# Sums of up-projection weights in five small steps and over more stages, and the next chunk's blocks among the last products

## The chip, the cores and the metric

One program on one core of a Trainium2 chip. The core has a matrix engine (TensorE, in the profile PE for its products and PEld for loading its weights), a vector engine (VectorE, DVE), a scalar engine (ScalarE, ACT), a third elementwise engine that also issues DMAs (GpSimd, POOL) and a sync engine (SyncE, SP) that here issues all loads of weights. The metric is the device time of one execution in microseconds (us); lower is better.

## The reference

One layer of a decoder for a prompt of 2048 rows and eight single sample rows, all in float32, width 1024. What matters, cut:

```python
def trunk_layer(x, ...):
    z = rmsnorm(x, g_mix) @ w_in            # pool 512 | q 512 | k 512 | v 512
    # group A: trailing means over 2, 4, 8, 16 rows; group B: differential attention, 4 heads, ALiBi
    o = attend(q, k, v, lam)                # softmax(q1 k1) - lam * softmax(q2 k2), times v
    x = x + concat([pool_out, rmsnorm(o)]) @ w_out
    x = x + cross_attn(rmsnorm(x, g_cross), mem_k, mem_v, wq_c, wo_c)     # 256 memory tokens
    f = conv_ffn(rmsnorm(x, g_ffn), conv_prefix, w_up, conv_w, conv_b, w_down)
    return x + f
def conv_ffn(h, prefix, w_up, conv_w, conv_b, w_down):
    up = h @ w_up                           # 1024 -> 2 * 2816, halves a | g
    c = causal_conv3(concat([prefix, up])) + conv_b
    return (silu(c_g) * c_a) @ w_down
```

The kernel also returns keys, values, memory keys and values, and the new pooling and convolution states.

## The kernel before, in words

**Numbers.** A float32 value is kept as two parts for the matrix engine, hi (a cast on ACT, `xhi`, `shi`, `whi`, L95 and L308) and lo (value minus hi, on DVE, `xlo`, `slo`, `wlo`, L96 and L311); a product is three matrix products, hi·hi, hi·lo and lo·hi.

**Stages.** The prompt is cut into four chunks of 512 rows and a few. In the profiled execution the stages follow each other so: memory keys and values and the first norm (0 to 90 us), input projection of chunks 0 and 1 (90 to 300), input projection of chunks 2 and 3 woven with the attention of chunks 0 and 1 (300 to 655), attention of chunks 2 and 3 woven with the output projection and first cross-attention work (655 to 1150), the rest of cross-attention together with the sample rows (1150 to 1640), and the feed-forward part, chunk by chunk (1640 to 3164, some 380 us a chunk).

**Feed-forward.** The 22 up-projections of a chunk go in groups of 4, 4, 4, 4, 4 and 2 (`GROUPS`). One up-projection (`ffn_up`, L1612 and L1614) yields an activation block and a gate block for two halves of the rows; instead of eight block products it makes seven, of sums and differences of blocks, in the manner of Strassen's algorithm. For this it needs (1) sums and differences of weight blocks, the same for all four chunks, and (2) seven blocks made from the chunk's normalized rows. The down-projections of a group (`down`, L1728, eight items of 12 products each) are spread among the products of the group behind it; those of a chunk's last group go among the first products of the next chunk.

**Weight sums** (`sums_items`). For each of the 22 up-projections a pair of tiles `wa`, `wg` (512 KB each) is loaded by SP (L1520), added and subtracted in four instructions on DVE (`add`, L1528 to L1531), split into hi and lo (`part`: per tile an ACT cast `shi`, L95, and a DVE subtraction `slo`, L96), and the four results are stored to DRAM tiles `s_d` by POOL's queue (L1540). The feed-forward part loads these back (`shl<-s_d`). A pair's load is recorded one pair ahead of its `add`. Eight pairs are woven into the input projection of chunks 0 and 1, fourteen into that of chunks 2 and 3 with the attention.

**Blocks of the next chunk** (`xop_items`). Seven items make the blocks: 14 tiles `xhi`/`xlo` of 128x512 and eight subtractions (L1572) on DVE. They stand behind the last up-projection of a chunk, in one run.

**What sets the order.** The order list at the end of the program is a list of items. `weave(main, extra, lo, hi)` spreads the items of `extra` over `main` by the cost of `main`'s items and the last number of each item of `extra`, from share `lo` to share `hi` of `main`. `drive` then records item by item, staging weights ahead (`look` says how many; load, then cast, then subtraction, L305, L308, L311). Each engine runs its instructions in the recorded order. All large tiles come from one pool of 41 buffers (`H`), so that a load on SP waits until the buffer that it takes is free, and every load behind it on SP waits with it. The loads of the attention's keys, values and queries (`K`, `V`, `Q`, L1073 to L1084) stand in the same queue.

## Time and profile before

| | us |
|---|---|
| median of three runs | 3166.14 |
| lowest and highest run | 3156.91, 3173.37 |
| the profiled execution | 3165.44 |
| its span, first to last instruction | 3163.7 |

The span lies 1.7 us below the time of the profiled execution. A row of the profile that names a group reads: line, engine, operation, tile written, tiles read and shape, then count, busy time, mean of one, and the idle time of the engine just ahead of these instructions with what ended it. A timeline row reads: start, duration, engine, line, operation, tiles, and in brackets the idle time before it with the instruction that ended it. The granted clock of TensorE (`PEclk`) is given as a share of full speed.

### The profile page before, as it was taken

The numbers are of one execution on the slowest core, as the hardware profiler recorded it, in microseconds if no ns is written. First come the engines' busy times: TensorE is split into PE (matmuls) and PEld (weight loads), VectorE is DVE, ScalarE is ACT, GpSimd is POOL, SyncE is SP. The second block draws the span as 40 slices with busy tenths as digits, with TensorE's granted clock in tenths as the row PEclk, the third lists the DMA queues.
The fourth block names the chain that finished last, engine by engine and source line by source line (L and its number), as shares of the span: only waits on it lengthen the run. The fifth ranks groups of instructions, "written<-read, shape, count | busy, mean of one in ns | idle before, by whom it ended". The sixth has DMA issues, their size and how long they took to land.

```text
span 3163.7 us, 52554 instructions
## 1 busy us (share of the span) xinstructions
PE 2958.2 (94%) x19806; PEld 2662.8 (84%) x19806; DVE 2244.5 (71%) x4032; ACT 1350.8 (43%) x2271; POOL 506.9 (16%) x961
## 2 busy tenths in 40 slices
PE   7999898879899998999989999999999999999998
PEld 6778787868889787679978989888898989899997
DVE  5744766556767668654568977887878777777777
ACT  5534444345665542333334343444434433443333
POOL 0244334321111115330000000000000010000100
PEclk9999999989999999999999999999999999999999
DMA  8797778843353356655449877677776786666762
GB/s 287 264 330 235 241 239 275 286 156 130 111 163 101 107 175 236 204 174 182 167 150 338 291 245 231 198 258 257 236 236 213 224 288 213 210 212 220 238 223 95
DMA packets 520513, 683.16 MB, mean 216 GB/s; under 512 B 27472, under 2 KB 342359, under 8 KB 520243
## 3 DMA queue, kind: packets, MB, share of 16 engines
q1 hardware_dynamic: 466525, 533.87, 52.2%
q0 software_dynamic: 39936, 135.17, 11.9%
q10 hardware_dynamic: 13798, 10.76, 1.0%
q8 instruction: 156, 2.56, 0.3%
q14 instruction: 98, 0.80, 0.1%
HBM read 549.12 MB, written 130.98 MB: 215 GB/s over the span
## 4 chain that ended last, share of the span: by engine, by line
PE 69%; DVE 9%; DMA 7%; issue 6%; ACT 2%; POOL 1%; SPq 0%; DVEq 0%; ACTq 0%; POOLq 0%
PE up L1612 14%; PE down L1728 14%; PE up L1614 7%; PE wo L484 4%; PE O L1164 3%; PE z L484 3%; PE sc L1112 3%; DMA wg<-in_w_up_dram 3%; PE upB L1612 2%; PE S L100 2%; PE S L102 2%; PE S L101 2%; PE vo L100 2%; PE vo L101 2%; PE vo L102 2%
## 5 line engine op out<-in xcount | busy, mean ns | idle before, releaser
L1728 PE MATMUL down<-act,whi 128*128 128x512 f32 (+1 forms) x1760 | 456.0, 353 | 11.8 <-ACT whi L308 8.4
L1612 PE MATMUL up<-xhi,shl 128*128 128x256 f32 (+1 forms) x2816 | 406.7, 286 | 5.1 <-ACT s L1627 1.8
L1612 PEld LDWEIGHTS up<-xhi,shl 128*128 128x128 f32 x2816 | 369.5, 189 | 37.1 <-ACT s L1627 11.2
L1666 ACT ACTIVATE cc<-Uf,vec 128x512 f32<-128x512 f32 (+1 forms) x176 | 144.0, 818 | 528.4 <-DVE Uf L1617 520.8
L311 DVE TENSOR_TENSOR wlo<-wraw,whi 128x1024 fp32r<-128x1024 f32 x256 | 308.6, 1218 | 38.8 <-ACT whi L308 26.4
L1728 PEld LDWEIGHTS down<-act,whi 128*128 128x128 f32 x1760 | 285.1, 189 | 43.3 <-ACT whi L308 9.3
L308 ACT CAST whi<-wraw 128x1024 fp32r<-128x1024 f32 x256 | 265.0, 1047 | 131.8 <-DMA wraw<-in_w_down_dram 30.0
L1728 PE MATMUL down<-act,wlo 128*128 128x512 f32 (+1 forms) x880 | 283.2, 353 | 7.5 <-DVE wlo L311 7.5
L1671 POOL COPY halo<-Uf 128x2 f32<-128x2 f32 x176 | 59.2, 336 | 1312.9 <-DVE Uf L1617 1273.1
L1130 ACT ACTIVATE T<-T,mn 128x1024 f32<-128x1024 f32 (+4 forms) x192 | 172.0, 897 | 143.0 <-DVE mn L1123 134.0
L1614 PE MATMUL up<-xlo,shl 128*128 128x256 f32 (+1 forms) x1408 | 225.1, 282 | 0.0
L1112 PE MATMUL sc<-K,Q 128*128 128x512 f32 (+5 forms) x640 | 178.0, 397 | 50.4 <-DVE mn L1123 44.8
L1612 PE MATMUL up<-xhi,whl 128*128 128x256 f32 (+1 forms) x1408 | 200.1, 285 | 5.1 <-DVE whl L330 3.0
L1612 PEld LDWEIGHTS up<-xhi,whl 128*128 128x128 f32 x1408 | 184.3, 190 | 13.9 <-DVE whl L330 5.2
L1614 PEld LDWEIGHTS up<-xlo,shl 128*128 128x128 f32 x1408 | 192.2, 189 | 0.2
L1674 DVE SCALAR_TENSOR_TENSOR cc<-Uf,vec,cc 128x512 f32<-128x512 f32 x176 | 131.5, 747 | 75.9 <-ACT cc L1666 75.8
L1617 DVE TENSOR_TENSOR Uf<-up,s 128x256 f32<-128x256 f32 (+1 forms) x264 | 111.6, 423 | 102.7 <-PE up L1614 100.7
L1728 PEld LDWEIGHTS down<-act,wlo 128*128 128x128 f32 x880 | 155.1, 189 | 31.7 <-DVE wlo L311 10.7
L330 DVE TENSOR_TENSOR whl<-wraw,whl 128x512 fp32r<-128x512 f32 x264 | 178.9, 684 | 0.2
L1112 PEld LDWEIGHTS sc<-K,Q 128*128 128x128 f32 x640 | 114.8, 201 | 73.1 <-DVE mn L1123 54.6
L484 PE MATMUL z<-h1hi,wlo 128*128 128x512 f32 (+1 forms) x480 | 163.7, 374 | 9.9 <-DVE mn L1123 5.4
L1732 DVE TENSOR_TENSOR xf<-xf,down 128x512 f32<-128x512 f32 (+1 forms) x240 | 135.0, 579 | 48.5 <-PE down L1728 46.7
(437 smaller groups left out, 7136.4 us busy)
## 6 DMA issues: line engine op xcount, KB each, us to landing
shl<-s_d SPq DMA_DIRECT2D x352, 512.0 KB
wraw<-in_w_up_dram SPq DMA_DIRECT2D x264, 256.0 KB
wraw<-in_w_down_dram SPq DMA_DIRECT2D x88, 512.0 KB
s_d<-shi POOLq DMA_DIRECT2D x44, 512.0 KB, 6.0
s_d<-slo POOLq DMA_DIRECT2D x44, 512.0 KB, 6.6
wraw<-in_w_in_dram SPq DMA_DIRECT2D x32, 512.0 KB
Q<-q_d SPq DMA_DIRECT2D x64, 256.0 KB
wraw<-in_w_out_dram SPq DMA_DIRECT2D x32, 512.0 KB
```

The costliest lines, as they stand in the source:

```text
L308: S.copy(self.hi[:, :1024], self.raw[:, :1024])
L311: V.tensor_tensor(self.lo[:, :1024], self.raw[:, :1024], f(self.hi[:, :1024]), ALU.subtract)
L330: V.tensor_tensor(self.hl[:, 512:1024], self.raw, f(self.hl[:, :512]), ALU.subtract)
L484: PE.matmul(out, w[wi][:, kt, :], kslice(z, kt, c0, n), start=i == 0, stop=i == 3 * KT - 1)
L1112: PE.matmul(ps[:, j * 512:j * 512 + w], v3(Q[c], 2)[:, z, self.t * P:(self.t + 1) * P], K[c][hf][:, c0:c0 + w], start=z == 0, stop=z == 1)
L1130: S.activation(tg[:, :mg], tg[:, :mg], AF.Exp, bias=mn[:, last:last + 1], scale=-1.0, accum_out=self.l[:, 2 * g + c:2 * g + c + 1])
L1612: PE.matmul(out, wi[:, k, :], xh[:, k], start=k == 0 and wi is wl, stop=False)
L1614: PE.matmul(out, wh[:, k, :], xl[:, k], start=False, stop=k == 3)
L1666: S.activation(cc[:, :w], U[:, 2:2 + w], AF.Identity, bias=vc(CB + nt), scale=vc(CWT + 2 * FT + nt))
L1674: V.scalar_tensor_tensor(cc[:, :CH], U[:, 1:1 + CH], vc(CWT + FT + nt), cc[:, :CH], ALU.mult, ALU.add)
L1728: PE.matmul(out, st["w"][0][wi][:, p, n0:n0 + P], act[:, z + c0:z + c0 + n], start=st_ and p == 0, stop=en and p == g - 1)
L1732: V.tensor_tensor(xx[:, c0:c0 + n], xx[:, c0:c0 + n], out, ALU.add)
```

## The change

1. In `sums_items` the load of a pair is no longer recorded one pair ahead, and a pair is five items in place of three: load, the first two additions, the last two, then the split of `wg` and the split of `wa`, each with weight 1.0.
2. The 22 pairs go to other places: five into the input projection of chunks 0 and 1, eight into that of chunks 2 and 3 with the attention, three into the attention of chunks 2 and 3, six into the last part of cross-attention.
3. The seven items that make the next chunk's blocks stand one each behind products of the chunk's last up-projection.
4. The down-projections of a group are laid elsewhere among the products of the next: 2, 3, 3, 0 in place of 3, 3, 1, 1, in a group's first up-projection behind its products 5 to 7, in others behind 2, 4 and 6; in a chunk's last group three, and then five behind the products.
5. The pool of six small tiles `Qt` (260 numbers a partition) is opened with the raw tiles, after the attention, and not from the start.

```diff
--- before.py
+++ after.py
@@ -55,7 +55,6 @@
     hp = ctx.enter_context(tc.tile_pool(name="hp", bufs=NBUF_H))
     sp = ctx.enter_context(tc.tile_pool(name="sp", bufs=6))
     tp = ctx.enter_context(tc.tile_pool(name="tp", bufs=16))
-    qp = ctx.enter_context(tc.tile_pool(name="qp", bufs=6))
     pa = ctx.enter_context(tc.tile_pool(name="pa", bufs=2, space=PSUM))
     pb = ctx.enter_context(tc.tile_pool(name="pb", bufs=4, space=PSUM))
     dr = ctx.enter_context(tc.tile_pool(name="dr", bufs=1, space=DRAM))
@@ -67,7 +66,7 @@
         return sp.tile([P, SW], dt, tag="S", name=name)
 
     def Qt(name):
-        return qp.tile([P, HW], F32, tag="q", name=name)
+        return rp[1].tile([P, HW], F32, tag="q", name=name)
 
     def Tn(name):
         return tp.tile([P, 8], F32, tag="t", name=name)
@@ -1521,28 +1520,30 @@
                 st[j] = wa, wg
             return item([], fn, 0, 1.0)
 
-        def add(j):
+        def add(j, i):
             def fn(_):
                 wa, wg = st[j]
                 a1, a2, g1, g2 = wa[:, :512], wa[:, 512:1024], wg[:, :512], wg[:, 512:1024]
-                V.tensor_tensor(g2, g1, g2, ALU.add)
-                V.tensor_tensor(g1, a1, g1, ALU.subtract)
-                V.tensor_tensor(a1, g2, a1, ALU.subtract)
-                V.tensor_tensor(a2, a2, a1, ALU.subtract)
-            return item([], fn, 0, 2.5)
-
-        def part(j):
+                if i:
+                    V.tensor_tensor(a1, g2, a1, ALU.subtract)
+                    V.tensor_tensor(a2, a2, a1, ALU.subtract)
+                else:
+                    V.tensor_tensor(g2, g1, g2, ALU.add)
+                    V.tensor_tensor(g1, a1, g1, ALU.subtract)
+            return item([], fn, 0, 1.0)
+
+        def part(j, i):
             def fn(_):
-                for i, t in enumerate(st.pop(j)):
-                    hi, lo = H("shi", F32R), H("slo", F32R)
-                    split(hi[:, :1024], lo[:, :1024], t[:, :1024])
-                    for z, p in enumerate((hi, lo)):
-                        ST.dma_start(s_d[j][:, i, z].rearrange("p s n -> p (s n)"), f(p[:, :1024]))
-            return item([], fn, 0, 2.5)
-
-        out = [load(js[0])]
+                t = st[j][i]
+                hi, lo = H("shi", F32R), H("slo", F32R)
+                split(hi[:, :1024], lo[:, :1024], t[:, :1024])
+                for z, p in enumerate((hi, lo)):
+                    ST.dma_start(s_d[j][:, i, z].rearrange("p s n -> p (s n)"), f(p[:, :1024]))
+            return item([], fn, 0, 1.0)
+
+        out = []
         for j in js:
-            out += [load(j + 1)] * (j + 1 in js) + [add(j), part(j)]
+            out += [load(j), add(j, 0), add(j, 1), part(j, 1), part(j, 0)]
         return out
 
     def k4(t):
@@ -1846,14 +1847,22 @@
         for g in GROUPS:
             if j == GROUPS[0]:
                 out.append(item([], ffn_open(c)))
-            last = j + g == NF and c < NCH - 1
+            last = j + g == NF
             for i in range(g):
                 u = ffn_up(c, j + i)
-                k = -(-(len(dn) - 2 * last) // min(g - i, 2 + (i == 0)))
+                k = (2, 1)[i] if last else (2, 3, 3, 0)[i]
                 d, dn = dn[:k], dn[k:]
-                for k, cuts in enumerate((u[:2], u[2:4], u[4:6], u[6:])):
-                    out += cuts + d[k:k + 1]
-            out += xops * last + dn
+                at = (5, 6, 7) if i == 0 else (2, 4, 6)
+                for k, up in enumerate(u):
+                    out.append(up)
+                    if last and i == g - 1:
+                        out += xops[k - 1:k] if k else []
+                    if k + 1 in at:
+                        out += d[:1]
+                        d = d[1:]
+            if last:
+                out += xops[6:]
+            out += dn
             dn = ffn_down(c, j, g)
             j += g
         if c == NCH - 1:
@@ -1871,6 +1880,7 @@
 
         dps.close()
         rp.append(ctx.enter_context(tc.tile_pool(name="rp", bufs=4)))
+        rp.append(ctx.enter_context(tc.tile_pool(name="qp", bufs=6)))
 
     half = p1_items((0, 1))
     pre = p0_items((0, 1))
@@ -1880,21 +1890,22 @@
     order += weave(weave(kv1, m0), n1[0][1][:3] + n1[1][0] + n1[0][1][3:], 0.1, 1.0)
     order += weave(weave(half[:12], m1), [item([], pool_load), item([], lambda_)] + n1[1][1], 0.2, 1.0)
     order += [look(3, 2, 1)]
-    main = weave(half[12:24] + [item([], pool_prep)] + half[24:-8], sums_items(range(8)), 0.0, 0.55)
-    order += weave(main, n1[2][0] + n1[2][1] + n1[3][0] + n1[3][1][:5] + [item([], att_table)], 0.65, 1.0)
+    order += weave(weave(half[12:24] + [item([], pool_prep)] + half[24:-8], sums_items(range(5)), 0.0, 0.6),
+                   n1[2][0] + n1[2][1] + n1[3][0] + n1[3][1][:5] + [item([], att_table)], 0.65, 1.0)
     order += att01[0] + weave(half[-8:], n1[3][1][5:])
     late = p1_items((2, 3))
     order += [look(4, 3, 2)]
-    order += weave(weave(late[:-10] + att23[0] + late[-10:], att01[1]), sums_items(range(8, NF)), 0.0, 0.9)
+    order += weave(weave(late[:-10] + att23[0] + late[-10:], att01[1]), sums_items(range(5, 13)), 0.05, 1.0)
     p3 = [p3_items(c) for c in range(NCH)]
     wo, n2, sc_, vo, n3 = zip(*p3)
-    order += weave(att23[1], wo[0] + weave(p0_items((2, 3)), n2[0], 0.0, 0.5) + sc_[0] + wo[1], 0.0, 1.0)
+    order += weave(weave(att23[1], wo[0] + weave(p0_items((2, 3)), n2[0], 0.0, 0.5) + sc_[0] + wo[1], 0.0, 1.0),
+                   sums_items(range(13, 16)), 0.0, 0.9)
     order += [item([], conv_state), item([], raw_open)]
     order += weave(vo[0], n2[1], 0.0, 0.9)
     order += weave(sc_[1] + wo[2], sample_items, 0.0, 0.95)
     order += weave(vo[1] + sc_[2][:8], merge(n2[2], sample_items2[:-2]) + sample_items2[-2:], 0.0, 0.55)
-    order += sc_[2][8:] + wo[3]
-    order += weave(vo[2], n2[3], 0.0, 0.9) + weave(sc_[3] + vo[3], n3[0] + xop_items(0), 0.4, 1.0)
+    order += weave(sc_[2][8:] + wo[3] + weave(vo[2], n2[3], 0.0, 0.9) + weave(sc_[3] + vo[3], n3[0] + xop_items(0), 0.4, 1.0),
+                   sums_items(range(16, NF)), 0.0, 0.85)
     xops = [xop_items(c) for c in range(1, NCH)] + [[]]
     order += [look(6, 3, 2)]
     order += weave(ffn_items(0, xops[0]), sc_items + n3[1], 0.02, 0.9)
```

SP in the input projection of chunks 2 and 3, before: `wraw` is a weight tile of the projection, `Q` the queries of an attention unit, `wa` and `wg` a pair of sums.

```order
L305 DMA wraw<-in_w_in_dram 128x8x128
L1084 DMA Q<-q_d_127 64x2x512 x4
L1520 DMA wa<-in_w_up_dram 128x8x128
L1520 DMA wg<-in_w_up_dram 128x8x128
L305 DMA wraw<-in_w_in_dram 128x4x256
L1520 DMA wa<-in_w_up_dram 128x8x128
L1520 DMA wg<-in_w_up_dram 128x8x128
L305 DMA wraw<-in_w_in_dram 128x4x256
L1084 DMA Q<-q_d_128 64x2x512 x4
```

SP at a place of the same stage, after:

```order
L304 DMA wraw<-in_w_in_dram 128x8x128
L1083 DMA Q<-q_d_124 64x2x512 x4
L304 DMA wraw<-in_w_in_dram 128x4x256
L1519 DMA wa<-in_w_up_dram 128x8x128
L1519 DMA wg<-in_w_up_dram 128x8x128
L304 DMA wraw<-in_w_in_dram 128x4x256
L1083 DMA Q<-q_d_125 64x2x512 x4
L304 DMA wraw<-in_w_in_dram 128x4x256
L1519 DMA wa<-in_w_up_dram 128x8x128
L1519 DMA wg<-in_w_up_dram 128x8x128
L304 DMA wraw<-in_w_in_dram 128x4x256
```

In the piece of before one weight tile lies between two pairs; in that of after two weight tiles and a query load lie between them.

DVE in the attention of chunks 2 and 3, before: L1123 is the masked row maximum of a score tile, L1137 to L1140 and L1147 scale the probabilities.

```order
L1139 RECIPROCAL rc<-l 128x2
L1140 TENSOR_TENSOR rc<-rc,lamv 128x2
L1123 ISA T,mn<-sc,Dt 128x1024
L1123 ISA mn 128x1
L1147 SCALAR_TENSOR_TENSOR T<-T,rc 128x1024
L1123 ISA T,mn<-sc,Dt,mn 128x640
L1123 ISA mn 128x1
L1147 SCALAR_TENSOR_TENSOR T<-T,rc 128x512
L1123 ISA T,mn<-sc,Dt 128x1024
L1123 ISA mn 128x1
L1137 TENSOR_TENSOR l<-l 128x2
L1123 ISA T,mn<-sc,Dt,mn 128x768
```

DVE at the same place, after (the lines of `add` are now L1528, L1529, L1531 and L1532, those of the attention one lower):

```order
L1139 TENSOR_TENSOR rc<-rc,lamv 128x2
L1122 ISA T,mn<-sc,Dt 128x1024
L1122 ISA mn 128x1
L1146 SCALAR_TENSOR_TENSOR T<-T,rc 128x1024
L1122 ISA T,mn<-sc,Dt,mn 128x640
L1122 ISA mn 128x1
L1146 SCALAR_TENSOR_TENSOR T<-T,rc 128x512
L1122 ISA T,mn<-sc,Dt 128x1024
L1122 ISA mn 128x1
L1532 TENSOR_TENSOR wg<-wa,wg 128x512
L1136 TENSOR_TENSOR l<-l 128x2
L1528 TENSOR_TENSOR wa<-wg,wa 128x512
```

The additions of a pair have come in between row maxima of this stage, one or two at a time.

DVE where chunk 0 of the feed-forward part ends, before: `xlo` and L1572 make the next chunk's blocks, L1732 adds a down-projection's result, `wlo` (L311) is the lo part of the weights of the next `down`.

```order
L1572 TENSOR_TENSOR x_18250<-x_18250,t_19720 128x2x256
L1572 TENSOR_TENSOR x_18251<-x_18251,t_19720 128x2x256
L1674 SCALAR_TENSOR_TENSOR cc<-Uf,vec,cc 128x512
L96 TENSOR_TENSOR xlo<-x_18250,xhi 128x2x256
L96 TENSOR_TENSOR xlo<-x_18251,xhi 128x2x256
L1675 SCALAR_TENSOR_TENSOR cc<-Uf,vec,cc 128x512
L1732 TENSOR_TENSOR xf<-xf,down 128x512
L311 TENSOR_TENSOR wlo<-wraw,whi 128x1024
```

DVE where the same blocks are made, after (`xlo` is L95, the subtractions L1573, `wlo` L310, `Uf` and `s` read a product's result, L1618):

```order
L95 TENSOR_TENSOR xlo<-x_18273,xhi 128x2x256
L310 TENSOR_TENSOR wlo<-wraw,whi 128x1024
L95 TENSOR_TENSOR xlo<-x_18274,xhi 128x2x256
L1618 TENSOR_TENSOR Uf<-up,s_19573 128x256
L1618 TENSOR_TENSOR s_19527<-up,s_19527 128x256
L1675 SCALAR_TENSOR_TENSOR cc<-Uf,vec,cc 128x512
L1573 TENSOR_TENSOR x_18271<-x_18273,x_18271 128x2x256
L1676 SCALAR_TENSOR_TENSOR cc<-Uf,vec,cc 128x512
L1573 TENSOR_TENSOR x_18272<-x_18274,x_18272 128x2x256
L95 TENSOR_TENSOR xlo<-x_18271,xhi 128x2x256
L310 TENSOR_TENSOR wlo<-wraw,whi 128x1024
L95 TENSOR_TENSOR xlo<-x_18272,xhi 128x2x256
```

Before, `wlo` stands behind the whole run of blocks; now two `wlo` stand among them, and so do the instructions that read the last products.

## Rows read from the trace of the kernel before

**Rows 1.** The page: engines, with busy time, share of the span and instructions.

```profile
PE 2958.2 (94%) x19806; PEld 2662.8 (84%) x19806; DVE 2244.5 (71%) x4032; ACT 1350.8 (43%) x2271; POOL 506.9 (16%) x961
```

**Rows 2.** By stage: window, length, busy PE, PEld, DVE, ACT, POOL, clock, DMA, GB/s.

```profile
90.00:300.00 210.00, 197.78 (x1077) 167.85 (x1076) 123.07 (x182) 91.94 (x142) 82.15 (x146) 0.98 0.87 294
300.00:655.00 355.00, 296.21 (x1932) 265.38 (x1931) 223.40 (x461) 160.35 (x304) 128.22 (x208) 0.93 0.80 256
655.00:1150.00 495.00, 464.74 (x3064) 414.26 (x3062) 339.64 (x616) 281.88 (x544) 82.87 (x88) 0.97 0.40 128
...
1390.00:1610.00 220.00, 207.59 (x1476) 195.18 (x1475) 113.09 (x160) 75.72 (x138) 6.62 (x11) 0.97 0.48 159
...
1650.00:3164.00 1514.00, 1466.21 (x10475) 1350.95 (x10473) 1187.88 (x2176) 597.81 (x919) 99.67 (x375) 0.99 0.70 233
```

**Rows 3.** Waits of PE, 300 to 655 us: total, times, longest.

```profile
PE sc L1112 <- DVE mn L1123: 29.1, 8, 13.3
PE z L484 <- DVE mn L1123: 5.4, 2, 4.5
...
PE sc L1112 <- DVE ql L729: 2.8, 1, 2.8
```

**Rows 4.** Waits of DVE, 300 to 655 us.

```profile
DVE wg L1528 <- DMA wg<-in_w_up_dram: 52.4, 11, 9.1
```

**Rows 5.** Timeline of SP, DVE, PE and ACT, single rows from 499 to 647 us.

```profile
499.16 0.63 SPq L1520 DMA_DIRECT2D wg<-in_w_up_dram  x1
511.29 0.69 DVE L1528 TENSOR_TENSOR wg<-wg 128x512 f32<-128x512 f32 x1 [7.17 <-DMA wg<-in_w_up_dram]
514.82 0.80 PE L484 MATMUL z<-h1hi,wlo 128*128 128x260 f32 x2 [4.55 <-DVE mn L1123]
...
595.71 0.47 SPq L1520 DMA_DIRECT2D wg<-in_w_up_dram  x1
603.91 0.69 DVE L1528 TENSOR_TENSOR wg<-wg 128x512 f32<-128x512 f32 x1 [9.14 <-DMA wg<-in_w_up_dram]
606.72 1.17 PE L1112 MATMUL sc<-K,Q 128*128 128x320 f32 x3 [7.01 <-DVE mn L1123]
...
638.67 1.04 ACT L308 CAST whi<-wraw 128x1024 fp32r<-128x1024 f32 x1 [13.56 <-DMA wraw<-in_w_out_dram]
646.01 1.22 PE L1112 MATMUL sc<-K,Q 128*128 128x512 f32 x2 [13.28 <-DVE mn L1123]
```

**Rows 6.** Groups of DVE, 100 to 650 us: the sums' work.

```profile
L96 DVE TENSOR_TENSOR slo<-wa,shi 128x1024 fp32r<-128x1024 f32 x22 | 27.4, 1245 | 13.7 <-ACT shi L95 13.6
...
L1528 DVE TENSOR_TENSOR wg<-wg 128x512 f32<-128x512 f32 x22 | 15.2, 689 | 62.6 <-DMA wg<-in_w_up_dram 62.6
```

**Rows 7.** Timeline: what now stands around two of the pairs.

```profile
440.04 0.37 SPq L305 DMA_DIRECT2D wraw<-in_w_in_dram  x1
465.36 1.01 DVE L1147 SCALAR_TENSOR_TENSOR T<-T,rc 128x768 f32<-128x768 f32 x1
...
578.26 0.93 PE L1153 MATMUL wT<-ident,T 128*128 128x128 f32 x7
584.71 0.35 DVE L1147 SCALAR_TENSOR_TENSOR T<-T,rc 128x128 f32<-128x128 f32 x1
```

**Rows 8.** Waits of PE, 90 to 300 us.

```profile
PE pool L100 <- DVE plo L96: 6.3, 3, 4.2
PE kT L749 <- ACT kf L739: 5.9, 1, 5.9
```

**Rows 9.** Waits of PE, 1640 us to the end; then its timeline where chunk 0 ends.

```profile
PE down L1728 <- ACT whi L308: 8.4, 4, 3.8
PE down L1728 <- DVE wlo L311: 7.5, 7, 1.5
...
2008.71 0.50 PE L1728 MATMUL down<-act,whi 128*128 128x512 f32 x1 [1.29 <-ACT whi L308]
2011.38 0.50 PE L1728 MATMUL down<-act,wlo 128*128 128x512 f32 x1 [1.48 <-DVE wlo L311]
```

## The prediction

> **What bounds the kernel now.** The page's list of engines comes first: the matrix engine is busy 2958 of 3164 us [rows 1], so at most some 206 us of idle time, and what a lowered clock costs, can be won. Where they lie is read from the busy times by stage [rows 2]. In the feed-forward part PE is idle 48 of 1514 us; from 655 to 1150 us it is 30 of 495, from 1390 to 1610 it is 12 of 220, from 90 to 300 it is 12 of 210. The outlier is 300 to 655 us, the projection of chunks 2 and 3 woven with the first attention: idle 59 of 355 us, and the lowest granted clock of the five, 0.93 of full. The engine is at a mix of its two levels there, and 0.07 x 355 = 25 us of full-clock time is not granted.
>
> Next, what PE waits for in that stage: DVE, with the row maximum `mn` 29.1 and 5.4 us and the query's lo part 2.8 us [rows 3], together 37.3. Then what DVE waits for: 52.4 us in 11 waits for a pair `wa`, `wg` that has not landed [rows 4], the largest wait of that engine here. The timeline joins the two. DVE sits 7.2 us at 511 us in front of the first addition, and 3.5 us later PE resumes after 4.6 us of idleness; at 604 us DVE sits 9.1 us, then PE comes back after 7.0 [rows 5]. The weight sums have nothing to do with the attention, but on an engine that runs in order the maxima of the scores stand behind them. One more hole has another cause: PE idles 13.3 us up to 646 us, when ACT has waited 13.6 us for a tile of `w_out` [rows 5]. Without it, 37.3 - 13.3 = 24.0 us of PE's waits stand behind DVE.
>
> **The change part by part.** The sum is made against the profiled execution (3165.4 us: span 3163.7 and 1.7 around it), 0.7 us under the median of the runs, so nothing is corrected between them.
>
> *Price of a pair.* Four additions of 0.689 us and two `slo` of some 1.23 us (the mean of `slo` of `wa` is 1.245) make 2.8 + 2.5 = 5.2 us of DVE [rows 6], wherever the pair stands. That does not change in sum: 22 pairs before, 22 after. What changes is where it lies, and how long DVE stands still in front of it.
>
> *(a) 90 to 300 us: 5 pairs where 8 stood.* DVE is busy 123 of 210 us and DMA 0.87 of the time, the most of the stages in [rows 2]; 3 MB less for each of three pairs (1 MB in, 2 MB out) relieve it by 9 of 62 MB (294 GB/s x 210 us). PE's waits here are 6.3 us for `plo` and 5.9 us for a key tile [rows 8]. I take half of those 12.2: **-6** us; bounds 0 and -11.
>
> *(b) 300 to 655 us: 8 pairs where 14 stood.* Two effects. First the waits. The load is no longer ahead by a pair, but the first addition now stands further behind its own load. For each of the eight pairs I looked up, in the trace of before, the instruction behind which the load can go in the new order (a buffer that comes free, or SP's load ahead of it) and the one behind which the first addition now stands. The eight distances run from 6 us (a buffer released by PE at 578 us, the addition behind DVE's instruction at 585 us) to 26 us (SP at 440, DVE at 465) [rows 7], and six of them are over 12. Against this stands what a pair takes under this load: 12.1 us from issue to first addition at 499 us and 8.2 us at 596 us [rows 5], say 10. Two pairs stay short of it, and the distances shrink when the stalls themselves vanish; I leave a third of the 52.4 us, by judgement. So of 24.0 us on PE two thirds go: -16. Lost clock goes along: the stage next to it, with less idle time, has 0.97 [rows 2], and I take half of that way, 0.02 x 355 = -7. Six pairs less are 31 us less DVE work of 223, which shortens waits such as the rest on `mn`: -4. Fewer pairs stand in SP's queue ahead of the next attention's keys and values and of the `w_out` tile, so the 13.3 us hole may become smaller: -3, a guess. Sum **-30**; bounds -10 (the loads are as late as before and only work moves) and -50 (all 24 us, the whole hole of 13.3 and 0.97 of clock).
>
> The Trainium skill, "DMA: Bandwidth & Descriptors", section "Anatomy of one DMA — SWDGE (gpsimd) path", fits a DMA by 2.0 us plus its bytes over 436 GB/s, for another issuing path than SP's: an estimate from it for the pair's 1 MB is 4.4 us. By that all eight distances would do, none of the waits would be left, and (b) would be -38. The trace disagrees: 8.2 and 12.1 us [rows 5].
>
> *(c) 655 to 1150 us: 3 pairs where none stood.* Here PE idles 30 us at 340 us of DVE work [rows 2]. In proportion 15.6 us more work cost 1.4 us; a wait like the mean of the 14 in (b), 52.4 / 14 = 3.7 us, of which PE felt 24.0 / 52.4, adds 1.7 for each pair. **+6**; bounds 0 (the DMA queue is at 0.40 here, so pairs land fast) and +20 (all of the work exposed, and one such wait more). Queued behind the additions are the row maxima and PE's score tiles behind them, which are the chain of this stage.
>
> *(d) 1390 to 1610 us: 6 pairs.* DVE is busy only 113 of 220 us and PE idles 12 [rows 2]. In proportion 31 us more work cost 3.4. **+3**; bounds 0 and, with six waits of 1.7, +14. Their stores end before the feed-forward part wants pair 16, which stands 16 up-projections into it.
>
> *(e) Feed-forward.* PE waits 8.4 us for `whi` and 7.5 for `wlo` of the down-weights [rows 9]. The largest come together where a chunk ends: at 2009 us `down` waits 1.3 and 1.5 us, since `wlo` stands behind the run of 14 block tiles on DVE. Three chunk ends like this are 8.3 us. The blocks now lie among the last products, `wlo` among them, and five of a group's eight down items follow to cover the tail. I take **-6**; bounds -16 (all of those waits) and +5 (blocks delay the instructions that empty the last products, as nothing in the trace of before has them there; the nearest row is the 1.3 us of one such wait, four times).
>
> The pool opened later costs nothing: its tiles are first used behind the new place.
>
> Sum: -6 - 30 + 6 + 3 - 6 = -33, so 3165.4 - 33 = **3132 us**. With the half-widths of the bounds (6, 20, 10, 7, 10) added as independent, some 26 us, its own range is 3106 to 3158.
>
> **The rivals.** *The pair comes no earlier.* With nothing fetched ahead, eight additions wait 6.5 us each in place of fourteen that waited 3.7 on the mean, and the 52.4 us stay; (b) keeps only the -4 and -3. For it: 11 of 14 additions waited even though they were fetched ahead [rows 4], and a pair takes 8 to 12 us. Against it: the distances above. It gives 3165 - 6 - 7 + 6 + 3 - 6 = 3155.
>
> The Trainium skill, "Trainium Kernel Development and Optimization", section "Best Practices", asks to double-buffer so that DMA overlaps compute; taking the load ahead away goes against it, and this rival is what comes of it. The trace bears the rule out half: being ahead did not keep DVE from waiting.
>
> *Slower: the moved pairs stop DVE where it is needed.* Nine pairs go to stages where none stood. If each holds DVE for a whole load (8.2 to 12.1, say 9.5 us) and its own 5.2 us of work, that is 14.7 x 9 = 132 us. With half of it on PE's path, +66 in place of the +9 of (c) and (d): 3165 - 42 + 66 = 3189. Half is near the 24.0 of 52.4 that PE felt in (b). It decides against the kernel from 42 / 132 = 32% on, and beyond 0.5% from 44% on. Against it: DMA is at 0.40 and 0.48 there instead of 0.80 [rows 2], and DVE has half its time free in the second.
>
> *The holes are filled by the next wait.* Where DVE comes earlier, PE in (b) next needs the projection's weights and queries by the same queue, and the stage is set by them at 0.80 DMA. Then (b) is -10: 3152.
>
> **How the numbers follow.** A measurement of this kernel can tell about 0.5%, 16 us: faster is below 3150, slower above 3182. My forecast has 0.62 (0.55 of it below 3150), the pair that comes no earlier 0.14, holes filled otherwise 0.12 (0.04 below 3150, since its spread reaches there), slower 0.08, and 0.04 is left for a gain beyond my own range, by more clock in (b). That makes faster 0.55 + 0.04 + 0.04 = 0.63, slower 0.08, within 0.29. For 8 in 10 the range takes the forecast's own and the two rivals near 3155, whose own spread I put at 8 us: 3105 to 3163.
>
> **What would show it.** (b): by stage, PE idle falls from 59 to about 40 in a stage some 30 us shorter, clock at 0.95, DVE's wait for `wg` near 17 us; if it is still near 50, the first rival holds. (c), (d): idle time of PE 655 to 1150 up by about 6; a wait of DVE for `wg` over 30 us there would be the slow rival. (e): `down` waits for `whi` and `wlo` at chunk ends gone. The prediction is wrong if the stage at 300 us does not shorten, or if the feed-forward part changes by more than 16 us.

## The result

The changed kernel takes 3121.65 us (median of four runs, 3116.27 to 3125.99), the kernel before on the same chips 3169.72 (four runs, 3156.91 to 3173.37). The ratio is 0.9855, interval 0.9821 to 0.9888: 1.45% faster, some 46 us. The forecast was 3132 in a range of 3105 to 3163. The profiled execution has a span of 3114.6 us, 49.1 less than before; it is the fastest of its four runs (3116.27, the others from 3121.59 on).

The sum came out near the forecast because two terms were missed in opposite directions. To see that, the two traces have to be cut at the same instruction, not at the same time. Between the first projection product, the first score product (`sc`), the first output-projection product (`wo`), the last attention product (`O`), the first up-projection product and the end:

| stretch | before | after | difference | forecast |
|---|---|---|---|---|
| to the first projection product | 65.6 | 67.1 | +1.5 | none |
| (a) projection, chunks 0 and 1 | 242.8 | 231.4 | -11.4 | -6 |
| (b) projection 2, 3 with attention 0, 1 | 383.0 | 349.1 | -33.9 | -30 |
| (c) attention 2, 3 | 457.2 | 475.7 | +18.5 | +6 |
| (d) cross-attention | 495.0 | 491.4 | -3.6 | +3 |
| (e) feed-forward | 1520.1 | 1499.9 | -20.2 | -6 |

The rows behind it are the busy times by stage: window, length, busy PE, PEld, DVE, ACT, POOL, granted clock, DMA share, GB/s. Before, (a), (b), (c) and (e):

```profile
65.60:308.40 242.80, 225.24 (x1237) 191.35 (x1236) 142.02 (x212) 113.45 (x178) 85.27 (x159) 0.96 0.82 278
308.40:691.40 383.00, 319.05 (x2075) 284.66 (x2073) 239.89 (x499) 174.24 (x337) 134.73 (x217) 0.92 0.77 247
691.40:1148.60 457.20, 432.11 (x2838) 385.61 (x2838) 318.54 (x573) 262.48 (x507) 75.12 (x77) 0.98 0.40 127
...
1643.60:3163.70 1520.10, 1472.61 (x10524) 1357.02 (x10522) 1189.42 (x2179) 598.18 (x920) 100.20 (x376) 0.99 0.70 233
```

After, the same stretches:

```profile
67.10:298.50 231.40, 221.27 (x1237) 188.62 (x1236) 129.93 (x196) 109.54 (x174) 79.83 (x149) 0.99 0.77 252
298.50:647.60 349.10, 309.84 (x2074) 280.96 (x2073) 214.56 (x465) 161.74 (x322) 118.77 (x191) 0.94 0.68 218
647.60:1123.30 475.70, 434.54 (x2839) 382.91 (x2838) 329.48 (x587) 267.80 (x513) 81.63 (x89) 0.97 0.43 141
...
1614.70:3114.60 1499.90, 1465.39 (x10524) 1352.97 (x10522) 1183.40 (x2179) 598.99 (x920) 112.39 (x376) 0.99 0.71 236
```

The counts of products agree, so the stretches hold the same work. In (b) PE's idle time fell from 64 to 39 us and its clock rose from 0.92 to 0.94. In (c) idle time rose from 25 to 41. How far such a length can be trusted: each is of one execution, and those of one kernel lie some 10 us apart (the changed one: 3116 to 3126). In four kernels of this study whose orders are alike up to there, (b) took 341.6 to 345.7 us and (a) 231.1 to 232.9; (c) took 455.1 and 457.7 in two whose orders are alike there. The last feed-forward chunk is firmer: 392.2 to 392.8 us in all eleven kernels with the change's feed-forward part, 398.3 to 401.0 in the three without it or with half of it.

The waits of (b) show the mechanism. DVE's wait for a pair and PE's waits, after:

```profile
DVE wg L1531 <- DMA wg<-in_w_up_dram: 7.5, 2, 6.5
```

```profile
PE sc L1111 <- DVE mn L1122: 17.2, 6, 8.3
PE z L483 <- DVE pps L708: 4.5, 1, 4.5
...
PE sc L1111 <- DMA Q<-q_d: 1.4, 1, 1.4
PE z L483 <- DVE mn L1122: 0.8, 1, 0.8
```

The first answers to [rows 4]: 52.4 us in 11 waits are 7.5 in two. For the row maxima, [rows 3] ends at 655 us, and before, (b) runs to 691.4. Cut like (b), the first of its rows is

```profile
PE sc L1112 <- DVE mn L1123: 34.3, 12, 13.3
```

and with the 5.4 us in front of `z`, 39.7 us before are 18.0 after. The largest hole left, 8.3 us, stands behind the same tile of `w_out` that made the 13.3 us hole in [rows 5]. After, ACT and PE there:

```profile
587.67 1.04 ACT L307 CAST whi<-wraw 128x1024 fp32r<-128x1024 f32 x1 [9.10 <-DMA wraw<-in_w_out_dram]
```

```profile
591.85 1.49 PE L1111 MATMUL sc<-K,Q 128*128 128x448 f32 x3 [8.32 <-DVE mn L1122]
```

### The profile page after: what moved, and what is told of

The parts are those of the page before. It is cut to its first block, busy times and chain, and to the rows that moved or that the text cites. A ratio compares the mean times of both kernels' runs of the same rounds, so it can differ in the third digit from the quotient of the medians.

```text
span 3114.6 us, 52466 instructions
## 1 busy us (share of the span) xinstructions
PE 2939.9 (94%) x19806; PEld 2650.3 (85%) x19806; DVE 2240.0 (72%) x4032; ACT 1351.9 (43%) x2271; POOL 516.2 (17%) x961
## 4 chain that ended last, share of the span: by engine, by line
PE 59%; DVE 8%; issue 4%; DMA 2%; ACT 2%; POOL 1%; DVEq 0%; ACTq 0%; POOLq 0%; SPq 0%
PE up L1613 15%; PE down L1729 15%; PE up L1615 7%; PE wo L483 3%; PE upB L1613 2%; PE S L99 2%; PE S L101 2%; PE S L100 2%; PE O L1163 2%; PE vo L99 1%; PE vo L100 1%; PE vo L101 1%; PE upB L1615 1%; PE sc L1111 1%; DVE T L1122 1%
## 5 line engine op out<-in xcount | busy, mean ns | idle before, releaser
L310 DVE TENSOR_TENSOR wlo<-wraw,whi 128x1024 fp32r<-128x1024 f32 x256 | 310.2, 1220 | 38.5 <-ACT whi L307 30.2
L1122 DVE CUSTOM_DVE_ANT_0 T<-sc,Dt 128x1024 f32<-128x1024 f32 (+7 forms) x128 | 125.8, 985 | 64.0 <-PE sc L1111 49.3
L1618 DVE TENSOR_TENSOR Uf<-up,s 128x256 f32<-128x256 f32 (+1 forms) x264 | 111.6, 423 | 83.0 <-PE up L1615 80.5
L327 ACT CAST whl<-wraw 128x512 fp32r<-128x512 f32 x264 | 155.2, 614 | 25.4 <-PE up L1615 6.4
```

Source lines behind the costliest of these rows:

```text
L310: V.tensor_tensor(self.lo[:, :1024], self.raw[:, :1024], f(self.hi[:, :1024]), ALU.subtract)
L327: S.copy(self.hl[:, :512], self.raw)
L1122: V.tensor_tensor_reduce(out, pin, din, -SLOPE[self.h], 3.0e38 if hf == 0 else mn[:, 0:1], ALU.add, ALU.min, mn[:, hf:hf + 1])
```

## The experiments

| run | us, median | ratio to before | interval |
|---|---|---|---|
| feed-forward edit alone | 3150.36 | 0.9952 | 0.9935 to 0.9968 |
| sums alone | 3142.64 | 0.9939 | 0.9912 to 0.9967 |
| changed, load ahead | 3129.01 | 0.9891 | 0.9866 to 0.9917 |
| changed, none in (c) | 3108.17 | 0.9820 | 0.9792 to 0.9849 |
| changed, places of before | 3132.42 | 0.9897 | 0.9863 to 0.9930 |
| before, blocks only | 3155.43 | 0.9971 | 0.9953 to 0.9989 |
| none in (c), three pairs in (e) | 3102.63 | 0.9810 | 0.9780 to 0.9841 |
| none in (c), DVE's additions there | 3106.34, one run | | |
| changed, lo in place | 3118.18 | 0.9854 | 0.9832 to 0.9875 |
| three pairs in (e), lo in place | 3100.35 | 0.9804 | 0.9777 to 0.9830 |
| none in (c), all engine work there | 3107.17 | 0.9822 | 0.9794 to 0.9851 |
| places 5, 6, 0, 6, 5, lo in place | 3112.62 | 0.9833 | 0.9813 to 0.9853 |

**The two edits apart.** The kernel before with the part of the diff in `ffn_items` alone:

> The kernel before with the feed-forward edit alone (places of the down-projections, blocks made among the last products). In the two traces the stage from the first up-projection product to the end went from 1520 to 1500 us, 20 us, where 6 were forecast. Theory: the edit itself does that, by the holes in front of the down-projections; then the stage is about 1500 us here too, the stages ahead of it are as before, and the run is near 3149 us. Rival: only the waits for the down-weights at the chunk ends (some 10 us) are the edit's, and the rest came with a higher granted clock that the quieter stages ahead of it left; then the stage is about 1510 us and the run near 3159.

And the changed kernel with that part of the diff taken back:

> The changed kernel with the feed-forward part of before: only the sums' new steps and places. If the two edits do not act on each other, the stages ahead of the feed-forward part are as in the changed kernel (first up-projection at about 1615 us instead of 1644), the feed-forward part takes 1520 us again, and the run is near 3137. If the sums' edit raised the clock of the later stage, the feed-forward part is about 1510 and the run near 3127.

Alone, the feed-forward edit made (e) 1500.9 us (1649.2 to 3150.1), the sums alone left it at 1521.6 (1615.3 to 3136.9) and had the first up-projection product at 1615.3. So by the traces 20 us are the feed-forward edit's own and 28 the sums'; the rival with the clock is out for both. The ratios of the runs give less, 15 and 19 us, for 46 of both together; their intervals, 10 to 21 us wide, leave room for either.

**Which half of the feed-forward edit.** The kernel before with the blocks made among the last products:

```diff
-                for k, cuts in enumerate((u[:2], u[2:4], u[4:6], u[6:])):
-                    out += cuts + d[k:k + 1]
-            out += xops * last + dn
+                xo = xops if last and i == g - 1 else []
+                for k, up in enumerate(u):
+                    out.append(up)
+                    out += xo[k - 1:k] if k else []
+                    if k in (1, 3, 5, 6):
+                        out += d[:1]
+                        d = d[1:]
+            if last:
+                out += xops[6:]
+            out += dn
```

> The kernel before, with only the next chunk's blocks made among the products of the last up-projection; the down-projections stay at their places of before. The whole feed-forward edit took 20 us off the stage from the first up-projection product to the end: 1520 to 1500. Theory: the blocks are less than half of it, 5 to 9 us in the chunk ends (three holes of about 2.8 us and lower clock), and the down-projections' places are the rest, as the forecast's bound of all waits for the down-weights says; the stage is 1511 to 1515. Rival: the blocks are nearly all of it: 1500 to 1504.

The theory held. (e) took 1513.2 us (1642.4 to 3155.6): the blocks are 7 of the 20, the places of the down-projections by subtraction 13. PE's waits in (e), blocks only:

```profile
PE down L1728 <- DVE wlo L311: 6.2, 7, 1.2
PE down L1728 <- ACT whi L308: 4.8, 1, 4.8
PE up L1612 <- DVE s L1617: 4.8, 7, 1.0
PE down L1728 <- DVE act L96: 3.4, 1, 3.4
```

and in the changed kernel:

```profile
PE up L1613 <- DVE s L1618: 8.3, 12, 1.2
PE up L1613 <- DVE whl L329: 4.9, 4, 3.4
PE down L1729 <- ACT whi L307: 3.1, 1, 3.1
```

The waits of `down` for weights, 15.9 us in [rows 9], are 11.0 with the blocks and 3.1 with both halves. The wait for `act`, 3.1 us behind a group's first products, is gone: two downs now stand where three stood, behind the fifth product and later. PE's idle time in (e) went from 47.5 to 43.6 and 34.5 us; the other 7 of 20 are in busy time (1472.6 to 1465.4). The clock, 0.99 in both rows, shows where they come from when it is read over the first 20 us of the chunks 1 to 3, where the last products of the chunk ahead have just run. Before:

```profile
2003.00:2023.00 20.00, 16.50 (x103) 14.58 (x102) 16.98 (x29) 8.13 (x13) 0.61 (x4) 0.91 0.46 146
2397.50:2417.50 20.00, 16.33 (x95) 14.11 (x94) 16.74 (x29) 8.20 (x13) 0.61 (x4) 0.83 0.41 140
2762.70:2782.70 20.00, 16.85 (x96) 14.60 (x95) 16.37 (x29) 8.29 (x13) 0.94 (x4) 0.83 0.47 149
```

After:

```profile
1975.80:1995.80 20.00, 19.30 (x142) 18.02 (x141) 15.51 (x29) 7.38 (x12) 1.47 (x4) 1.00 0.84 281
2362.60:2382.60 20.00, 19.32 (x142) 18.06 (x141) 15.55 (x29) 7.29 (x13) 1.47 (x4) 1.00 0.87 280
2722.00:2742.00 20.00, 19.32 (x141) 18.18 (x140) 15.36 (x32) 7.41 (x12) 1.47 (x4) 1.00 0.83 272
```

Before, the holes at the chunk ends took 8.6 us of full-clock time along (0.09 + 0.17 + 0.17 of 20 us each); after, nothing there. With the blocks alone the three clocks are 1.00, 0.91 and 0.91, so 3.6 us.

**Steps or places, and the load ahead.** Two kernels take one part of the sums' edit back. The changed kernel with the places of before:

```diff
-    ... sums_items(range(5)), 0.0, 0.6 ...
+    ... sums_items(range(8)), 0.0, 0.55 ...
...
-    ... sums_items(range(5, 13)), 0.05, 1.0)
+    ... sums_items(range(8, NF)), 0.0, 0.9)
...
-                   sums_items(range(13, 16)), 0.0, 0.9)
+                   [], 0.0, 0.9)
...
-                   sums_items(range(16, NF)), 0.0, 0.85)
+                   [], 0.0, 0.85)
```

> The changed kernel with the pairs at the places of before (8 in the projection of chunks 0 and 1, 14 in the stage with the attention, none later), still in five steps and not loaded ahead. It tells the steps from the places. In the changed kernel the stage from the first score product to the first output-projection product took 349 us, before 383. Theory: the places do it, 14 pairs of 5.2 us of DVE and 3 MB are too many for that stage however they are cut, and each load now has less time to its addition; DVE's waits for the pairs are 30 us or more and the stage is 370 to 385. Rival: the small steps do it, since no additions stand in one run in front of the row maxima; then the waits are under 20 us and the stage 350 to 360.

The theory held: (b) took 373.1 us, in the slowest of four runs (3138.9 us), and DVE waits there as it did before:

```profile
DVE wg L1531 <- DMA wg<-in_w_up_dram: 43.9, 11, 10.0
```

Of the 34 us of (b), 24 go with the places and 10 with the rest of the sums' edit, the small steps and the load no longer ahead. In (a), eight pairs in small steps took 241.6 us, hardly less than the 242.8 of before.

The changed kernel with each load one pair ahead:

```diff
-        out = []
+        out = [load(js[0])]
-            out += [load(j), add(j, 0), add(j, 1), part(j, 1), part(j, 0)]
+            out += [load(j + 1)] * (j + 1 in js) + [add(j, 0), add(j, 1), part(j, 1), part(j, 0)]
```

> The changed kernel, but each pair's load is recorded one pair ahead again; the five steps and the places stay. Theory: what took DVE's waits for the pairs away (62.6 to 8.0 us) is the distance between load and first addition, which comes from spreading fewer pairs over more work; then a load still further ahead leaves these waits under 15 us and the run within 0.5% of the changed kernel, 3106 to 3137. Rival: loads ahead were themselves the harm, since they take two buffers early and stand in SP's row before the attention's and the projection's loads; then the waits for the pairs or for weights come back by 20 us or more and the stage from the first score product to the first product of the output projection goes from 349 to 360 us or more.

The run is 3129.0 us, its ratio not told apart from the changed kernel's, and (b) is 351.4, so loads ahead were not the harm there. Its trace is of the fastest of its four runs, 3117.2 us, 11 under the next, so its stages flatter it. The waits for pairs were 21.6 us in all, not under 15, and two stages moved: (a) from 231.4 to 240.3, (c) from 475.7 to 467.2. In (a) the reason is to be seen. Busy times by 10 us, the kernel before:

```profile
150.00:160.00 10.00, 7.57 (x26) 6.08 (x27) 8.88 (x12) 3.98 (x6) 3.36 (x7) 0.83 1.08 380
160.00:170.00 10.00, 8.83 (x38) 6.67 (x37) 8.35 (x12) 6.23 (x9) 4.85 (x9) 1.00 1.04 351
200.00:210.00 10.00, 4.51 (x20) 3.35 (x18) 2.21 (x5) 5.09 (x11) 4.59 (x9) 0.85 0.97 369
210.00:220.00 10.00, 9.57 (x39) 7.88 (x40) 2.75 (x8) 1.55 (x3) 5.24 (x11) 0.80 1.04 399
```

and the changed one:

```profile
150.00:160.00 10.00, 6.95 (x29) 5.33 (x30) 9.83 (x14) 5.05 (x8) 3.72 (x8) 1.00 1.01 326
160.00:170.00 10.00, 10.00 (x45) 8.10 (x44) 8.78 (x12) 5.81 (x8) 6.01 (x12) 1.00 1.09 380
200.00:210.00 10.00, 10.00 (x49) 8.14 (x49) 2.24 (x4) 1.91 (x4) 5.39 (x10) 1.00 0.48 115
```

Before, the holes of [rows 8] (4.2 us in front of 152 us, 5.9 in front of 210) are each followed by a clock of 0.80 to 0.85 over ten us. In the changed kernel none at the first place is longer than 2.0 us, at full clock, and the second is gone. With the load ahead the longest is 4.5 us again. PE's waits there (total, times, longest, 67 to 300 us), the changed kernel and then with the load ahead:

```profile
PE pool L99 <- DVE plo L95: 4.5, 3, 2.0
```

```profile
PE pool L99 <- DVE plo L95: 8.0, 3, 4.5
```

So some 7 of the 11 us of (a) were idle time (17.6 to 10.1 us), and the other 4, in busy time, go with the clock that the holes took along (0.96 to 0.99). Neither half of the edit does this alone: five pairs with the load ahead leave (a) at 240.3, eight in small steps without it at 241.6.

**What three pairs cost in (c).** The changed kernel with these pairs moved to the last part of cross-attention:

```diff
-                   sums_items(range(13, 16)), 0.0, 0.9)
+                   [], 0.0, 0.9)
...
-                   sums_items(range(16, NF)), 0.0, 0.85)
+                   sums_items(range(13, NF)), 0.0, 0.85)
```

> The changed kernel with the three pairs of the attention of chunks 2 and 3 moved to the last part of cross-attention (nine there). From the first output-projection product to the last attention product the changed kernel takes 476 us, before took 457. Theory: the three pairs are the cost of that stage, by their work on DVE between the row maxima; without them it takes about 458, the last part of cross-attention takes 255 to 260, and the run is near 3106. Rival: the stage is longer since it starts with less done or with other holes, whoever works on DVE; then it stays at 470 or more and the run at 3120.

(c) fell from 475.7 to 455.1: the pairs are the cost, some 20 us for 15.6 us of DVE work, of which 12.8 lie in (c) and the rest ahead of it. (d) rose from 491.4 to 505.1 us; laid product on product (each product of one trace against the same product of the other), 6 of these 14 us are lost ahead of the first of the nine pairs and 8 behind it. By the ratios the run still gained some 11 us, with intervals that overlap. What of a pair costs that much? In place of the three pairs, first DVE's work alone, then all engine work, on data that nobody uses, without loads and stores:

```diff
...
+        def work(size, m):
+            def fn(_):
+                t = H("dw")
+                for _i in range(m):
+                    V.tensor_tensor(t[:, :size], Dt[:, :size], Dt[:, size:2 * size], ALU.add)
+            return item([], fn, 0, 1.0)
+        return [w for _ in range(n) for w in (work(512, 2), work(512, 2), work(1024, 1), work(1024, 1))]
...
-                   [], 0.0, 0.9)
+                   dve_items(3), 0.0, 0.9)
```

> The kernel without pairs in the attention of chunks 2 and 3 (nine in the last part of cross-attention), with plain additions on DVE put in that stage: as many and as large as those of three pairs, on data that nobody uses, in steps, without loads, casts, subtractions of a cast or stores. Without pairs the stage takes 455 us, with three pairs 474 to 476. Theory: DVE's work between the row maxima is the price, 15.6 us of work for 20 us of time; then this stage is 470 to 476. Rival: the price is of the loads, casts on ACT, stores and buffers; then it is 455 to 460.

```diff
...
+        def part(_):
+            hi, lo = H("dhi", F32R), H("dlo", F32R)
+            split(hi[:, :1024], lo[:, :1024], Dt[:, :1024])
+        return [item([], w, 0, 1.0) for _ in range(n) for w in (none, adds, adds, part, part)]
...
-                   [], 0.0, 0.9)
+                   engine_items(3), 0.0, 0.9)
```

> The kernel without pairs in the attention of chunks 2 and 3, with all engine work of three pairs put there at the very places that it has in the changed kernel (four additions, two casts on ACT and two lo parts on DVE a pair, on data that nobody uses), without loads and stores. Without pairs the stage takes 455 us, with DVE's work alone 462, with three whole pairs 476; writing the lo part in place moved a wait for buffers from DVE to ACT and took nothing off (480). Theory: the casts between the exponentials on ACT, with DVE's lo parts behind them, are what is missing; then the stage is 470 to 478. Rival: loads, stores and the buffers that a pair holds until its stores have ended are what is missing; then it is 458 to 466.

Busy times of (c) in the kernel with none and in these two:

```profile
644.10:1099.20 455.10, 431.68 (x2840) 385.39 (x2838) 318.55 (x574) 261.73 (x505) 74.94 (x77) 0.98 0.39 127
```

```profile
642.00:1103.70 461.70, 434.11 (x2840) 386.47 (x2838) 331.25 (x589) 262.70 (x507) 75.41 (x77) 0.97 0.39 126
```

```profile
640.10:1106.50 466.40, 434.46 (x2838) 386.09 (x2838) 333.37 (x591) 267.74 (x513) 74.18 (x77) 0.97 0.39 125
```

Both theories fell: DVE's work is 6.6 us of the 20, with casts and lo parts it is 11.3 (a little over the rival's 466, under the theory's 470), and some 9 us are left for loads, stores and the time that a pair holds its buffers. With 2.6 us between two kernels of like order, each of these parts is good to some 3 us. Both kernels take buffers of the pool too, only for a shorter time, and in the second DVE waits for one:

```profile
DVE dlo L95 <- PE wo L483: 4.7, 1, 4.7
```

As whole runs the two are no slower than the kernel with none (3106.3 in a single run and 3107.2 against 3108.2): what (c) lost came back in (d), 500.7 and 495.6 us for the same nine pairs against 505.1, all of it ahead of the first of these pairs. Why (d) starts faster there is open, and so the prices above are those of the stage and not of the run. One wait for a buffer is plain in the changed kernel's timeline: DVE stands 6.8 us in front of a lo part, until a product of the output projection gives a buffer back, and PE has two holes behind it. Laid product on product on the kernel with none, 7 of the 20 us are lost between 1058 and 1068 us, at this place.

```profile
1057.97 1.23 DVE L95 TENSOR_TENSOR slo<-wa,shi 128x1024 fp32r<-128x1024 f32 x1 [6.80 <-PE wo L483]
```

```profile
1060.88 1.43 PE L1111 MATMUL sc<-K,Q 128*128 128x384 f32 x4 [3.01 <-DVE mn L1122]
...
1065.33 0.90 PE L1152 MATMUL wT<-ident,T 128*128 128x128 f32 x3 [3.03 <-DVE T L1146]
```

So the lo part was written over the sum's own tile, which saves two buffers a pair:

```diff
-                hi, lo = H("shi", F32R), H("slo", F32R)
+                hi, lo = H("shi", F32R), t.bitcast(F32R)
```

> The changed kernel, but the lo part of a sum is written over the sum's own tile, so a pair takes four large buffers in place of six. In the changed kernel DVE stands 6.8 us at 1058 us in front of a lo part, until a product of the output projection frees a buffer, ACT 3.9 us likewise in front of a hi part, and PE has two holes of 3.0 us right behind. Plain additions on DVE explained only some 7 us of the 20 that three pairs cost in the stage from the first output-projection product to the last attention product (476 us with them, 455 without). Theory: waits for buffers in the rows of DVE and ACT are a good part of the rest; then those waits are gone and the stage is 464 to 470. Rival: the buffers wait moves to the loads on SP or the casts on ACT are the price; then the stage stays at 472 or more.

DVE's wait was gone, ACT kept its own in front of a hi part:

```profile
ACT shi L94 <- PE wo L483: 3.9, 1, 3.9
```

and (c) took 479.6 us: PE's idle time is 39.2 us for 41.2, and its busy time 440.5 for 434.5, at a clock of 0.96 for 0.97. The theory fell here too. (b) fell by 12 us to 337.2, but the run is no faster (0.9854).

What the last 9 us of the 20 are is open. The load ahead took 8.5 off (c), and it did not do so by the buffer, for which DVE waits there as long as in the changed kernel:

```profile
DVE slo L95 <- PE wo L483: 6.7, 1, 6.7
```

Laid product on product, all of the 8.5 us lie between 836 and 843 us of the changed kernel. There DVE waits for a cast `h2hi` of cross-attention's rows, the row maxima stand behind its lo part `h2lo`, and PE has two holes:

```profile
834.38 1.23 DVE L281 TENSOR_TENSOR h2lo<-x,h2hi 128x1024 fp32r<-128x1024 f32 x1 [6.12 <-ACT h2hi L277]
```

```profile
836.86 1.20 PE L1111 MATMUL sc<-K,Q 128*128 128x512 f32 x4 [2.35 <-DVE mn L1122]
842.17 1.12 PE L1152 MATMUL wT<-ident,T 128*128 128x128 f32 x4 [4.11 <-DVE T L1146]
```

On ACT this cast stands ahead of two exponentials in the changed kernel and behind them in the one with the load ahead. So the order of the stage's own instructions may be the cause of these 8.5 us as well as the loads, and no run tells them apart.

**A better kernel.** As none in (c), with three of the nine pairs in the first feed-forward chunk:

```diff
-                   sums_items(range(13, NF)), 0.0, 0.85)
+                   sums_items(range(13, 19)), 0.0, 0.85)
...
-    order += weave(ffn_items(0, xops[0]), sc_items + n3[1], 0.02, 0.9)
+    order += weave(weave(ffn_items(0, xops[0]), sc_items + n3[1], 0.02, 0.9), sums_items(range(19, NF)), 0.05, 0.6)
```

> As the kernel with none in the attention of chunks 2 and 3, but three of its nine pairs of the last part of cross-attention moved on into the first 60% of the first chunk of the feed-forward part. With nine pairs the two stages from the last attention product to the first up-projection product took 243 and 263 us, with six 237 and 255; the first chunk took 360. Theory: the feed-forward part has PE full and DVE at 0.82, and in products that wait for no DVE chain three pairs cost less than 10 us; then the chunk takes 362 to 370 and the run is 3100 to 3106. Rival: DVE there empties every product, and three pairs cost their whole 16 us and more: chunk at 376 or more, run at 3112 or more.

The theory held: (d) is 489.3 us, the chunk 364.8 against 360.4 with none (360.1 to 362.7 in eight kernels), and the ratio to before is 0.9810, where the changed kernel has 0.9855; the intervals overlap a little. With lo in place it is the same within its interval, though (b) went to 338.9 us:

> The kernel with no pair in the attention of chunks 2 and 3, six in the last part of cross-attention and three in the first chunk of the feed-forward part (run at 3102.6 us), with the lo part written over the sum's own tile. Without pairs where buffers were short it should gain little: 3097 to 3105, by earlier loads. If buffers bound the projection stage too, the stage from the first score product to the first output-projection product falls from 346 to under 340 and the run is under 3096.

Two more pairs moved from (b) to that chunk, so five there, went too far:

```diff
-    ... sums_items(range(5, 13)), 0.05, 1.0)
+    ... sums_items(range(5, 11)), 0.05, 1.0)
...
-    ... sums_items(range(13, 19)), 0.0, 0.85)
+    ... sums_items(range(11, 17)), 0.0, 0.85)
...
-    ... sums_items(range(19, NF)), 0.05, 0.6)
+    ... sums_items(range(17, NF)), 0.03, 0.65)
```

> As the last, with the places 5, 6, 0, 6 and 5 pairs (input projection of chunks 0 and 1; of chunks 2 and 3 with the attention; attention of chunks 2 and 3; last part of cross-attention; first feed-forward chunk) in place of 5, 8, 0, 6, 3. From 14 to 8 pairs in the stage with the attention cost 373 and 349 us, 4 us a pair; three pairs in the first feed-forward chunk cost 4 us together. Theory: DVE has room in the feed-forward part, so two pairs moved there gain 8 us and cost 3 to 4: 3093 to 3100. Rival: DVE in that chunk is then at more than nine tenths, and the products wait for it: the chunk goes from 365 to 375 or more and nothing is gained.

The rival's times held: (b) gained 2 us where 8 were hoped for (338.9 to 337.1), and the chunk grew from 366.8 to 380.6. Its reason did not, since DVE is busy 0.84 of the chunk and not over nine tenths. The chunk's row, with three pairs and with five:

```profile
1591.70:1958.50 366.80, 353.80 (x2413) 320.22 (x2412) 310.43 (x513) 152.44 (x236) 25.05 (x103) 0.99 0.83 280
```

```profile
1590.00:1970.60 380.60, 357.03 (x2414) 321.56 (x2413) 320.04 (x525) 156.75 (x240) 29.36 (x111) 0.98 0.85 286
```

The largest of PE's waits there with five is not DVE but `shl`, 6.5 us for sums that come back from DRAM:

```profile
PE up L1613 <- DMA shl<-s_d: 6.5, 3, 3.4
```

## Why the prediction was right, and where it was not

(b), the main term, was right in mechanism and size: -34 for -30. The waits for pairs fell further than was left (7.5 us, not 17), the clock rose by 0.02 as forecast, and the `w_out` hole shrank by 5.0 us for a guess of 3. The size is in part luck: 10 of the 34 us go with the small steps and the load no longer ahead, for which the sum had no term of its own. The first rival, that pairs not fetched ahead come as late as before, is refuted: the places alone bring their waits back (43.9 us). The rule beside it, in the Trainium skill, "Trainium Kernel Development and Optimization", section "Best Practices", to double-buffer, did not decide here: with and without the load ahead the runs are not told apart, and by the traces (a) is better without by 9 us, (c) better with by 8.5. The rival that the next wait fills the holes is out too: (b) fell by 34 us, not by 10, and PE waits 1.4 us for queries there.

(a) was mis-sized: -11.4 for -6. The step took half of two waits of PE and no clock; both holes went, and each had cost a lowered clock behind it as well. It came out just past the bound of -11. Its reason, fewer bytes, is not enough by itself: with the same five pairs loaded ahead (a) is 240.3 us, only 2.5 under before.

(c) was mis-sized: +18.5 for +6. The step priced DVE's work in proportion to idle time, 1.4 us, and added 5 us for waits like those of (b). No such wait came: no wait of DVE for a pair is in the trace of (c). DVE's work by itself cost 4 to 7 us, by the kernel with its additions alone and the two with none. Missing was also that a pair brings casts, buffers and stores into a stage whose score chain runs through ACT and DVE in order, and that a full pool stops DVE itself: a wait for a buffer, on the engine and not on SP, at the place of 7 of the 20 us. The Trainium skill, "Perfetto Trace Analysis", section "Tensor Engine Instruction (MATMUL, LD_WEIGHTS)", says that ACT and DVE are strictly first in, first out; the trace agrees, 6.8 us in front of `slo` with the maxima behind it.

(d) had the wrong sign by a little: -3.6 for +3. Six pairs have no price there that can be told: (d) takes 495.0 to 497.7 us in the four kernels with none, 489.3 to 495.2 in the seven with six. Nine cost some 8 us more than six.

(e) was the step that failed: -20.2 for -6, past the bound of -16, and by the prediction's own words a change of over 16 us there made it wrong. The blocks were sized right (7 us), though 3 of the 7 are clock. That the largest waits for weights stand where a chunk ends is so for `wlo` alone; the longest for `whi`, 3.8 us, stands at 2590 us inside a chunk, stays with the blocks alone (4.8 us) and goes with the new places. The new places of the down-projections were described and not priced: the bound took all of `down`'s waits for weights, but not the wait for `act`, and no clock. As in (a), a hole was priced by its length alone, and the clock behind the holes at the chunk ends was worth another 8.6 us.

The slow rival (nine pairs stop DVE for 14.7 us each) did not come about: DVE waits for no pair in (c), a pair costs some 7 us there by other ways, and nothing that can be told in (d).

So the time lies 10 us under the forecast and inside its range by (b) being right and by luck: (c) missed by 12 us upwards, (a), (d) and (e) by 5, 7 and 14 downwards. The sum was better than its terms.

## What to carry to other kernels

Side work on an in-order engine is not priced by its busy time. A pair with 5.2 us of DVE work cost nothing that could be told where DVE was half idle, 1 to 2 us among products that did not wait for it, and some 7 us of the stage between the links of a softmax chain. Lay it first where the main chain does not run through that engine, and stop adding when the stage starts to grow: three pairs in the first feed-forward chunk cost some 4 us, two more another 14. Price a hole of the matrix engine with the clock that it takes along, and not by its length alone. Cut two traces at the same instructions before comparing them, or one stage's gain hides another's loss.

## What the runs showed of the hardware

A hole of PE can cost more than its length: in the input projection, behind holes of 4.2 and 5.9 us the granted clock was 0.80 to 0.85 over ten us, and at the first of these places, behind holes of at most 2.0 us, it stayed at 1.00 (rows above). Shorter holes took clock too where two came close together: 1.3 and 1.5 us at the end of the first chunk [rows 9], with 0.91 over 20 us. A pair of 512 KB loads took 8 to 12 us from issue to use in the stage at 0.80 DMA [rows 5]; with five pairs in the first feed-forward chunk, at 0.85 DMA, PE waited 6.5 us for other loads.
